# Order of the feed-forward units, layout of the attention values and place of the RWKV solve in a two-layer hybrid trunk

## The chip, the cores and the metric

The kernel runs on one core of a Trainium2 chip. The metric is the device time of one execution in microseconds (us). Three executions of the kernel before took 2157.81, 2156.45 and 2154.91 us; their median, 2156.45 us, is the time before.

The engines are named as in the profile: PE is TensorE (matmuls), PEld its weight loads, DVE is VectorE, ACT is ScalarE, POOL is GpSimd, SP is the engine that issues nearly all DMAs. Each engine takes its own instructions in a fixed order that is set when the program is built.

## The reference

Two layers; in each, two feed-forward half steps stand around a token mixer, and a small gated embedding closes the layer. The sequence has 512 tokens, the model width is 1024.

```python
def swiglu(x, w_in, w_out):                      # w_in 1024 x 5632, w_out 2816 x 1024
    gate, up = jnp.split(x @ w_in, 2, axis=-1)
    return (jax.nn.silu(gate) * up) @ w_out

# attention: 8 query heads, 2 key/value heads of 64, a window of 128 tokens, one sink logit per head
probs = jax.nn.softmax(jnp.concatenate([scores, sink], axis=-1), axis=-1)[..., :-1]
out = jnp.einsum('bnhgqk,bnkhd->bnqhgd', probs.astype(v.dtype), vb)

# RWKV-7, per token and head: S_t = S_{t-1} diag(w_t) + (S_{t-1} a_t) b_t^T + v_t k_t^T, y_t = S_t r_t

for l in range(DEPTH):
    x = x + 0.5 * rms_norm(swiglu(rms_norm(x, ln_ffn1_pre[l]), ...), ln_ffn1_post[l])
    mix = token_mixing(...)          # concat(attention, mLSTM, RWKV-7) @ w_out
    x = x + rms_norm(mix, ln_mix_post[l])
    x = x + 0.5 * rms_norm(swiglu(rms_norm(x, ln_ffn2_pre[l]), ...), ln_ffn2_post[l])
    gate = jax.nn.sigmoid(rms_norm(x, ln_ple_pre[l]) @ w_ple_gate[l])
    x = x + rms_norm(gate * (p[l] @ w_ple_proj[l]), ln_ple_post[l])
```

## The kernel before

**Precision.** A large product is three matmuls (`mm3`, L167 to L171): both factors are split into a high part (a rounding copy on ACT, L141) and the rest (a subtraction on DVE, L142), and high by high, high by low and low by high are added up. Every weight block that arrives from HBM therefore costs an ACT and a DVE pass before PE can use it.

**Feed-forward.** `ffn` (L334) computes gate and up for 22 units of 128 columns with a seven-product scheme (Strassen-Winograd over two halves of the model width and of the tokens): a unit needs sums of its weights (L386, L388, L389 on DVE), their splits (w75, w63 and w4, L390 to L392), the products 6, 7, 5, 3 and 4 on PE (L396 to L408, twelve matmuls of 128x256 each) and sums of the results on DVE (L397 to L413). The products 1 and 2, of the gate alone, are done for the first eight units (m below G = 8) ahead of all units, in `one` and `two`; for the fourteen others they stand in `gate` (L379), 24 matmuls and one more split (w12) per unit. The eight are called early units here, the fourteen late units. The loop L424 takes the units in order of their number. The result of four units fills one buffer `hs`, which `ffn_out` reads.

**Token mixing.** `weave` (L686) steps four generators in the order of the string PLAN: A attention, R the RWKV scan with its triangular solve, M the mLSTM, P the projection of its output gate. In A, `softmax` (L1360) leaves exponentials, divides them by their sum (L1387 on DVE for two heads, L1389 on POOL for the two others), and `values` (L1391) turns each block of 128 keys with four PE transposes (L1399), copies it to SBUF and multiplies: the 64 value columns are the stationary operand, the four heads' 512 columns move (L1405). The output is channel-major and is split into the high and low part for the out projection (L716 to L719). In R, `rwkv_solve` (L887) begins with `invert_merge` (L1037); its first products carry the name pt0 (L1056).

**Order.** The program is built under a scheduler that places every instruction by a simulated timeline, so neighbours in an engine's queue come from different units or generators; waits are semaphores.

## Time and profile before

| | us |
|---|---|
| median of three runs | 2156.45 |
| the profiled execution, its own time | 2158.23 |
| its span, first to last instruction | 2156.5 |
| PE busy | 2103.3 |
| PE weight loads busy | 1953.4 |
| DVE busy | 1697.9 |

The stages of the first layer in the span: feed-forward 1 to about 370 us, projections of the mixer to 500, the weave to 627, the out projection to 669, feed-forward 2 to about 1010, the gated embedding to 1080. The second layer has the same order and ends at 2156.5. The busy time of PE is a union of overlapping matmuls, so the pace of PE is read from the number of matmuls in a stretch, and its pauses from the difference between a stretch and its busy time.

### The profile page before, as it was taken

The numbers are of one execution on the slowest core, as the hardware profiler recorded it, in microseconds if no ns is written. First come the engines' busy times: TensorE is split into PE (matmuls) and PEld (weight loads), VectorE is DVE, ScalarE is ACT, GpSimd is POOL, SyncE is SP. The second block draws the span as 40 slices with busy tenths as digits, with TensorE's granted clock in tenths as the row PEclk, the third lists the DMA queues.
The fourth block names the chain that finished last, engine by engine and source line by source line (L and its number), as shares of the span: only waits on it lengthen the run. The fifth ranks groups of instructions, "written<-read, shape, count | busy, mean of one in ns | idle before, by whom it ended". The sixth has DMA issues, their size and how long they took to land.

```text
span 2156.5 us, 39845 instructions
## 1 busy us (share of the span) xinstructions
PE 2103.3 (98%) x16256; PEld 1953.4 (91%) x16256; DVE 1697.9 (79%) x2909; ACT 1015.6 (47%) x1685; POOL 219.9 (10%) x369
## 2 busy tenths in 40 slices
PE   7999999999999999999999999999999999999998
PEld 7999999898778999999889999998887789999996
DVE  8999977655767999977699999765557589999774
ACT  6444434446545444434564444345464464444343
POOL 1000011031211000011100000111412110000121
PEclk9999999999999999999999999999999999999999
DMA  5332124321042323225233222242220423222241
GB/s 215 120 116 99 70 87 153 116 65 55 21 155 71 137 99 118 69 79 182 92 108 125 111 79 93 86 169 94 61 64 2 157 88 138 100 97 79 82 147 66
DMA packets 72679, 219.10 MB, mean 102 GB/s; under 512 B 16304, under 2 KB 17328, under 8 KB 72496
## 3 DMA queue, kind: packets, MB, share of 16 engines
q1 hardware_dynamic: 72208, 216.03, 28.5%
q8 instruction: 128, 2.10, 0.4%
q10 hardware_dynamic: 288, 0.52, 0.1%
q14 instruction: 55, 0.45, 0.1%
HBM read 209.71 MB, written 6.82 MB: 100 GB/s over the span
## 4 chain that ended last, share of the span: by engine, by line
PE 84%; DVE 7%; ACT 4%; DMA 2%; issue 2%; POOL 1%; SPq 0%; DVEq 0%; POOLq 0%; ACTq 0%
PE y L496 21%; PE p L169 12%; PE p L171 12%; PE p L170 12%; PE pkrv L169 1%; PE pkrv L171 1%; PE pkrv L170 1%; DVE w L142 1%; PE y L171 1%; PE y L169 1%; PE y L170 1%; PE pgt L169 1%; PE pgt L171 1%; PE pgt L170 1%; PE po L1405 1%
## 5 line engine op out<-in xcount | busy, mean ns | idle before, releaser
L169 PE MATMUL p<-xh,w 128*128 128x256 f32 x1408 | 400.2, 286 | 14.1 <-DVE gates L397 5.8
L171 PE MATMUL p<-xh,w 128*128 128x256 f32 x1408 | 397.0, 284 | 3.7 <-DVE w L142 3.6
L170 PE MATMUL p<-xl,w 128*128 128x256 f32 x1408 | 398.7, 284 | 0.3 <-DVE xl L142 0.2
L169 PE MATMUL p<-tx,w 128*128 128x256 f32 x1056 | 294.2, 282 | 5.6 <-DVE ws L386 4.1
L170 PE MATMUL p<-tx,w 128*128 128x256 f32 x1056 | 292.1, 280 | 0.0
L171 PE MATMUL p<-tx,w 128*128 128x256 f32 x1056 | 289.8, 280 | 0.5 <-DVE w L142 0.5
L169 PEld LDWEIGHTS p<-xh,w 128*128 128x128 f32 x1408 | 268.8, 192 | 19.0 <-DVE gates L397 6.6
L171 PEld LDWEIGHTS p<-xh,w 128*128 128x128 f32 x1408 | 268.5, 192 | 5.1 <-DVE w L142 5.1
L170 PEld LDWEIGHTS p<-xl,w 128*128 128x128 f32 x1408 | 269.7, 192 | 1.0 <-DVE xl L142 0.9
L141 ACT ACTIVATE w<-ws 128x1024 fp32r<-128x1024 f32 x176 | 185.5, 1056 | 128.7 <-PE p L171 98.7
L142 DVE TENSOR_TENSOR w<-ws,w 128x1024 fp32r<-128x1024 f32 x176 | 214.0, 1217 | 19.4 <-ACT w L141 19.0
L169 PEld LDWEIGHTS p<-tx,w 128*128 128x128 f32 x1056 | 199.4, 189 | 8.1 <-ACT w L141 6.7
L170 PEld LDWEIGHTS p<-tx,w 128*128 128x128 f32 x1056 | 199.2, 189 | 0.0
L171 PEld LDWEIGHTS p<-tx,w 128*128 128x128 f32 x1056 | 196.3, 188 | 0.9 <-DVE w L142 0.7
L496 PE MATMUL y<-wo,hq 128*128 128x256 f32 x1536 | 193.3, 283 | 0.0
L496 PEld LDWEIGHTS y<-wo,hq 128*128 128x128 f32 x1536 | 186.4, 190 | 0.8
L141 ACT ACTIVATE w<-wr 128x512 fp32r<-128x512 f32 (+1 forms) x156 | 126.9, 816 | 108.8 <-PE p L171 61.5
L496 PE MATMUL y<-ws_r,h 128*128 128x256 f32 x672 | 158.3, 379 | 0.0
L142 DVE TENSOR_TENSOR w<-wr,w 128x512 fp32r<-128x512 f32 (+1 forms) x156 | 141.9, 915 | 9.9 <-ACT w L141 8.9
L532 POOL TENSOR_TENSOR tb<-tb,ln_ffn_post 128x512 f32<-128x512 f32 x16 | 24.4, 1558 | 1143.2 <-ACT junk L198 1143.2
L496 PEld LDWEIGHTS y<-ws_r,h 128*128 128x128 f32 x672 | 121.4, 189 | 13.8
L386 DVE TENSOR_TENSOR ws<-wr 128x1024 f32<-128x1024 f32 x88 | 107.0, 1216 | 0.1
(432 smaller groups left out, 4612.3 us busy)
## 6 DMA issues: line engine op xcount, KB each, us to landing
wr<-in_w_ffn_in SPq DMA_DIRECT2D x176, 512.0 KB, 4.1
ws_r<-in_w_ffn_out SPq DMA_DIRECT2D x56, 512.0 KB, 3.3
wo_r<-in_w_ffn_out SPq DMA_DIRECT2D x32, 512.0 KB, 3.3
w_r<-in_w_ffn_in SPq DMA_DIRECT2D x20, 512.0 KB, 3.8
pkrv_r<-in_w_rw SPq DMA_DIRECT2D x16, 512.0 KB, 3.5
wpg_r<-in_w_ple_gate SPq DMA_DIRECT2D x16, 512.0 KB, 4.0
xd<-x SPq DMA_DIRECT2D x8, 512.0 KB, 2.7
x<-xd SPq DMA_DIRECT2D x8, 512.0 KB, 3.5
```

The lines of the kernel that those rows point to most:

```text
L141: self.nc.scalar.activation(hi, src, AF.Copy)
L142: (eng or self.nc.vector).tensor_tensor(lo, src, hi.bitcast(F32), ALU.subtract)
L169: mm(out, a[0], b[0], start=first, stop=False, skip_group_check=shared)
L170: mm(out, a[0], b[1], start=False, stop=False, skip_group_check=shared)
L171: mm(out, a[1], b[0], start=False, stop=last, skip_group_check=shared)
L386: v_.tensor_tensor(sx.rearrange("p (i c) -> p i c", i=2), r[:, :, lo], r[:, 1].rearrange("p (i c) -> p i c", i=2), ALU.add)
L496: nc.tensor.matmul(banks[n][:, u], x, y, start=n not in seen, stop=last and i == len(todo) - 1, skip_group_check=True)
L532: (g_ if not h or QL[0] == "1" else v_).tensor_tensor(tb, tb, gain[:, h * 512:h * 512 + 512], ALU.mult)
L1405: mm(po[0][hr[g]], kv[:, t - (t + b) % 2, 2 + g], sb, start=b == 0, stop=b == nb - 1)
```

## The change

Three things change. In `ffn`, the units run in the order UNITS, which mixes early and late ones, and inside a unit the products 7 and 5 come first; the split w75 follows its sum directly. In attention, the exponentials are no longer divided: the probabilities are now the stationary operand and the 64 value columns move, one matmul per head and key block, the output is token-major, DVE multiplies it by the reciprocal sums while it leaves PSUM, and PE turns each token tile back before the split. In the RWKV solve, the first products of the first half (pt0) are issued only after the last matmul of the first tile of the mLSTM values, gates and forget gates (`pvif`).

```diff
+UNITS = (0, 1, 2, 8, 9, 3, 10, 4, 11, 12, 5, 13, 6, 14, 15, 7, 16, 17, 18, 19, 20, 21)
...
-        mm(out, a[1], b[0], start=False, stop=last, skip_group_check=shared)
+        return mm(out, a[1], b[0], start=False, stop=last, skip_group_check=shared)
...
+            w75 = self.wsplit(sx, "w75")
             v_.tensor_tensor(sy[:, lo], sx[:, hi], r[:, 0, lo], ALU.add)
             v_.tensor_tensor(sy[:, hi], sy[:, lo], r[:, 0, hi], ALU.add)
-            sx, sy = self.wsplit(sx, "w75"), self.wsplit(sy, "w63")
+            w63 = self.wsplit(sy, "w63")
...
-            product(6, self.cut(sy, lo), pc[:, L])
+            product(7, self.cut(w75, lo), pb[:, P])
+            product(5, self.cut(w75, hi), pb[:, Q])
+            product(6, self.cut(w63, lo), pc[:, L])
             v_.tensor_tensor(a[:, Q], pc[:, L], a[:, Q if m < G else P], ALU.add)
-            product(7, self.cut(sx, lo), pb[:, P])
-            product(5, self.cut(sx, hi), pb[:, Q])
...
-        for m in range(NM):
+        for m in UNITS:
...
+            if name == "pvif" and t == 0:
+                self.held = end.ins
...
-                    self.split(self.yh[:, 0:4, ts], self.yl[:, 0:4, ts], y.rearrange("p (a i) -> p a i", a=4),
-                               self.pl_(1))
+                    self.main, self.aux, self.chain = cycles["A"]
+                    pt = self.aux_tile("pat").rearrange("p (a i) -> p a i", a=4)
+                    for j in range(4):
+                        self.nc.tensor.transpose(pt[:, j], y[:, j * 128:(j + 1) * 128], self.ident)
+                    self.split(self.yh[:, 0:4, ts], self.yl[:, 0:4, ts], pt)
...
+        def first(zq):
+            if q:
+                return prod(zq, None, "pt0")
+
+            with self.tc.issue_after(self.held):
+                return prod(zq, None, "pt0")
...
-            nc.scalar.activation(t0, prod(zq, None, "pt0"), AF.Copy)
+            nc.scalar.activation(t0, first(zq), AF.Copy)
...
-            n = 4 - int(PL[4])
-            for i in range(n):
-                v_.tensor_scalar_mul(pr[:, i, :nk], pr[:, i, :nk], sm[:, i:i + 1])
-            if n < 4:
-                g_.tensor_tensor(pr[:, n:, :nk], pr[:, n:, :nk], sm[:, n:, None].to_broadcast([128, 4 - n, nk]), ALU.mult)
+            rc[g] = sm
...
-                mm(po[0][hr[g]], kv[:, t - (t + b) % 2, 2 + g], sb, start=b == 0, stop=b == nb - 1)
-            if g:
-                y = self.ytile()
-                a_.activation(y, po[0], AF.Copy)
-                ys.append(y)
+            for i in range(4):
+                for b in range(nb):
+                    mm(po[0][:, i, g], sbs[:, b, i * 128:(i + 1) * 128], kv[:, t - (t + b) % 2, 2 + g],
+                       start=b == 0, stop=b == nb - 1)
+
+            v_.tensor_tensor(ys[t].rearrange("p (a g d) -> p a g d", a=4, g=2)[:, :, g], po[0][:, :, g],
+                             rc[g][:, :, None].to_broadcast([128, 4, 64]), ALU.mult)
```

**DVE in the first feed-forward stage.** The queue of DVE from the split w75 of unit 2 on, before. The names carry buffer numbers: w75, w63, w4 and w12 are splits of weights, ws the sums of weights, wr the weights as they arrive, and gates, up and h the results of a unit.

```order
L142 TENSOR_TENSOR w75_681<-ws_676,w75_681 128x1024
L405 TENSOR_TENSOR gates_259<-p63_518,up_521 128x256
L142 TENSOR_TENSOR w63_684<-ws_677,w63_684 128x1024
L386 TENSOR_TENSOR ws_765<-wr_762 128x1024
L406 TENSOR_TENSOR up_521<-p75_519,up_521 128x256
L142 TENSOR_TENSOR w4_777<-wr_762,w4_776 128x512
L405 TENSOR_TENSOR gates_259<-p63_605,up_608 128x256
L388 TENSOR_TENSOR ws_766<-ws_765,wr_762 128x512
L409 TENSOR_TENSOR up_521<-up_521,p4_520 128x256
L397 TENSOR_TENSOR gates_259<-p63_691,gates_259 128x256
L142 TENSOR_TENSOR w75_770<-ws_765,w75_770 128x1024
```

The same place now (the lines of the changed kernel are a few numbers higher; L144 is the split, L388 the first sum):

```order
L144 TENSOR_TENSOR w75_679<-ws_676,w75_679 128x1024
L403 TENSOR_TENSOR up_608<-p75_606,gates_259 128x512
L408 TENSOR_TENSOR gates_259<-p63_518,up_521 128x256
L388 TENSOR_TENSOR ws_795<-wr_762 128x1024
L144 TENSOR_TENSOR w63_684<-ws_677,w63_684 128x1024
L409 TENSOR_TENSOR up_521<-p75_519,up_521 128x256
L144 TENSOR_TENSOR w4_807<-wr_762,w4_806 128x512
L408 TENSOR_TENSOR gates_259<-p63_605,up_608 128x256
L391 TENSOR_TENSOR ws_796<-ws_795,wr_762 128x512
L144 TENSOR_TENSOR w12_767<-wr_762,w12_767 128x1024
L412 TENSOR_TENSOR up_521<-up_521,p4_520 128x256
```

After unit 2 the weights that arrive in wr_762 were those of unit 3, an early one; now they are those of unit 8, whose split w12 for the gate's own products stands in the queue.

**PE at the first tile of pvif, first layer.** Before, the four groups of eight small transposing products pt0 stand between the first matmuls of pvif, the last of them ahead of its thirteenth (po is the attention's value product, pqt and pkt its transposes).

```order
L171 MATMUL pvif<-pvif,xl 128x264
L1050 MATMUL pt_6041<-ident,arena 64x64 x4
L1348 MATMUL pqt<-ident,arena 128x128 x4
L1050 MATMUL pt_6051<-ident,arena 64x64 x3
L169 MATMUL pvif<-pvif,xh 128x264
L1050 MATMUL pt_6051<-ident,arena 64x64 x4
L1405 MATMUL po<-arena 64x512
L1356 MATMUL pkt<-ident,arena 128x128 x2
L1050 MATMUL pt_6051<-ident,arena 64x64
L170 MATMUL pvif<-pvif,xh 128x264
```

At the same place now, none of them is left:

```order
L173 MATMUL pvif<-pvif,xl 128x264
L1363 MATMUL pqt<-ident,arena 128x128 x4
L171 MATMUL pvif<-pvif,xh 128x264
L1418 MATMUL po<-arena 128x64 x4
L1371 MATMUL pkt<-ident,arena 128x128 x2
L172 MATMUL pvif<-pvif,xh 128x264
```

The first eight stand behind the twenty-fourth matmul of pvif now, in one piece:

```order
L172 MATMUL pvif<-pvif,xh 128x264
L173 MATMUL pvif<-pvif,xl 128x264
L1058 MATMUL pt_6083<-ident,arena 64x64 x8
L171 MATMUL pvif<-pvif,xh 128x264
L172 MATMUL pvif<-pvif,xh 128x264
```

What moved is the start of the solve: past the first tile of pvif with its first eight products, and past all four tiles with the next eight, which stand behind the last matmul of pvif.

**PE at the end of the solve's first half, first layer.** Before (pz, pwt and pzq belong to the solve, pss to the mLSTM, pT and pS to attention):

```order
L1050 MATMUL pz<-arena 64x64 x16
L902 MATMUL pwt<-arena,at 64x64 x8
L1405 MATMUL po<-arena 64x512 x2
L1348 MATMUL pqt<-ident,arena 128x128 x4
L902 MATMUL pwt<-arena,at 64x64 x8
L910 MATMUL pzq<-x,arena 64x64 x16
L1196 MATMUL pss<-arena 128x128 x2
```

And now:

```order
L1058 MATMUL pz<-arena 64x64 x16
L1418 MATMUL po<-arena 128x64 x8
L1363 MATMUL pqt<-ident,arena 128x128 x4
L910 MATMUL pwt<-arena,at 64x64 x16
L918 MATMUL pzq<-x,arena 64x64 x15
L1211 MATMUL pss<-arena 128x128 x2
```

Two value matmuls of 512 columns became eight of 64, and the solve's last product pzq stands between the same neighbours as before.

## Rows read from the trace of the kernel before

**Rows 1.** The page's first and fourth part: busy time, share of the span and instructions of each engine, and the chain that ended last by engine.

```profile
PE 2103.3 (98%) x16256; PEld 1953.4 (91%) x16256; DVE 1697.9 (79%) x2909; ACT 1015.6 (47%) x1685; POOL 219.9 (10%) x369
...
PE 84%; DVE 7%; ACT 4%; DMA 2%; issue 2%; POOL 1%; SPq 0%; DVEq 0%; POOLq 0%; ACTq 0%
```

**Rows 2.** Busy time by stretch: the early units of the four feed-forward stages, then a stretch of late units. Columns: stretch, its length, then each engine's busy us and instructions, the granted clock of PE, the DMA share and GB/s.

```profile
60.00:125.00 65.00, 60.88 (x507) 60.00 (x506) 63.69 (x99) 28.54 (x36) 0.00 (x0) 1.00 0.31 115
700.00:760.00 60.00, 57.36 (x474) 56.26 (x473) 57.90 (x89) 27.45 (x33) 0.00 (x0) 1.00 0.35 126
1100.00:1190.00 90.00, 84.89 (x688) 83.62 (x689) 85.69 (x126) 42.84 (x58) 0.00 (x0) 0.98 0.34 124
1766.00:1835.00 69.00, 67.11 (x557) 66.09 (x556) 67.38 (x101) 32.29 (x40) 0.00 (x0) 1.00 0.38 138
162.00:216.00 54.00, 54.00 (x457) 54.00 (x456) 50.34 (x76) 24.62 (x33) 0.00 (x0) 1.00 0.27 99
```

**Rows 3.** Who PE waited for in the stretch 60 to 125 us: us in total, times, longest.

```profile
PE p L169 <- DVE ws L386: 1.9, 1, 1.9
PE p L169 <- DVE gates L397: 1.4, 1, 1.4
PE p L171 <- DVE w L142: 0.8, 1, 0.8
```

**Rows 4.** Busy time by stretch: the weave of the first and of the second layer; columns as in rows 2.

```profile
500.00:626.90 126.90, 120.69 (x1234) 95.62 (x1232) 84.10 (x270) 67.26 (x176) 24.51 (x28) 0.99 0.11 35
1568.20:1691.30 123.10, 121.02 (x1225) 94.42 (x1224) 82.55 (x264) 66.37 (x175) 22.75 (x27) 0.99 0.11 32
```

**Rows 5.** Who PE waited for in the weave of the first layer.

```profile
PE pwt L1182 <- DVE arena L1224: 1.2, 1, 1.2
PE pst L954 <- POOL arena L948: 1.0, 1, 1.0
...
PE py L962 <- DVE x L911: 0.6, 1, 0.6
PE pT L1399 <- DVE arena L1387: 0.6, 1, 0.6
```

**Rows 6.** The timeline of DVE in the stretch 60 to 125 us: start, duration, line and operation.

```profile
82.14 0.68 DVE L389 TENSOR_TENSOR ws<-ws,wr 128x512 f32<-128x512 f32 x1
82.74 1.22 DVE L386 TENSOR_TENSOR ws<-wr 128x1024 f32<-128x1024 f32 x1
83.87 0.41 DVE L397 TENSOR_TENSOR gates<-p,gates 128x256 f32<-128x256 f32 x1
84.21 0.41 DVE L409 TENSOR_TENSOR up<-up,p 128x256 f32<-128x256 f32 x1
```

**Rows 7.** Groups of DVE splits: count, then busy us and mean ns of one, then the idle time of DVE just before them and what ended it.

```profile
L142 DVE TENSOR_TENSOR w<-ws,w 128x1024 fp32r<-128x1024 f32 x176 | 214.0, 1217 | 19.4 <-ACT w L141 19.0
L142 DVE TENSOR_TENSOR w<-wr,w 128x512 fp32r<-128x512 f32 (+1 forms) x156 | 141.9, 915 | 9.9 <-ACT w L141 8.9
```

**Rows 8.** Busy time by stretch around a pause of PE in the second layer, then the same pause in the first layer; columns as in rows 2.

```profile
1148.00:1151.00 3.00, 1.10 (x9) 0.90 (x8) 3.00 (x6) 1.38 (x2) 0.00 (x0) 1.00 0.11 26
1151.00:1154.40 3.40, 3.40 (x18) 3.40 (x18) 3.38 (x6) 0.00 (x0) 0.00 (x0) 0.51 0.72 286
82.00:85.40 3.40, 1.50 (x13) 1.44 (x13) 3.40 (x6) 1.06 (x1) 0.00 (x0) 1.00 0.41 149
```

**Rows 9.** The timeline of PE at one pair of value products: start, duration, line, operation and shape.

```profile
547.15 1.93 PE L1405 MATMUL po<-arena 128*64 128x512 f32 x4
549.01 0.33 PE L1348 MATMUL pqt<-ident,arena 128*128 128x128 f32 x1
```

**Rows 10.** Groups of the attention's instructions that go, and the nearest one to what comes on DVE; columns as in rows 7.

```profile
L1405 PE MATMUL po<-arena 128*64 128x512 f32 x56 | 27.5, 605 | 0.0
L1387 DVE TENSOR_SCALAR arena<-arena,sm 128x256 f32<-128x256 f32 (+1 forms) x32 | 17.8, 598 | 0.3
L1389 POOL TENSOR_TENSOR arena<-arena,sm 128x512 f32<-128x512 f32 (+1 forms) x16 | 15.7, 980 | 111.6 <-DVE sm L1384 74.6 <-DVE vg L1118 35.5 <-ACT ysq L989 1.5
L405 DVE TENSOR_TENSOR gate<-p,up 128x256 f32<-128x256 f32 x56 | 23.4, 417 | 7.5 <-PE p L171 7.4
```

**Rows 11.** The timeline of PE's weight loads at a matmul of 16 columns (pgm) and at the projection after it.

```profile
532.24 0.30 PEld L1132 LDWEIGHTS pgm<-vg,arena 128*128 128x128 f32 x2
532.46 0.19 PEld L170 LDWEIGHTS pog<-pog,xh 128*128 128x128 f32 x1
532.57 0.19 PEld L171 LDWEIGHTS pog<-pog,xl 128*128 128x128 f32 x1
```

**Rows 12.** The chain of waits in the weave of the first layer: one group of four transposes there.

```profile
544.38 0.59 PE pT L1399 x4
```

**Rows 13.** The timeline of DVE just ahead of the first wait of rows 5; columns as in rows 6.

```profile
559.10 1.40 DVE L1387 TENSOR_SCALAR arena<-arena,sm 128x256 f32<-128x256 f32 x2
560.42 0.48 DVE L1224 COPY arena<-pnum 128x130 f32<-128x130 f32 x2
```

**Rows 14.** The timeline of PE at the solve's start in the first layer, pt0 and the products after it; columns as in rows 9.

```profile
502.15 0.45 PE L1050 MATMUL pt<-ident,arena 64*64 64x64 f32 x8
...
509.58 0.44 PE L1050 MATMUL pgi<-arena,x 64*64 64x64 f32 x6
520.48 1.02 PE L1050 MATMUL pgi<-arena,x 64*64 64x64 f32 x26
```

More of the change, by code (lines that the diff above doesn't have):

```diff
@@ L345, in ffn @@
         right = {1: plain(k1, L), 2: plain(k2, L), 3: plain(k2, H), 4: tx[2], 5: plain(k1, H), 6: tx[0], 7: tx[1]}
-        hs = []
+        hs = {}
         lo, hi = slice(0, 512), slice(512, 1024)
@@ L403, in unit @@
                 v_.tensor_tensor(a[:, P], pa[:, H], a[:, P], ALU.add)
-            product(3, self.cut(sy, hi), pc[:, H])
+            product(3, self.cut(w63, hi), pc[:, H])
             v_.tensor_tensor(a[:, Q], pc[:, H], b[:, Q], ALU.add)
@@ L409, in unit @@
             v_.tensor_tensor(b[:, P], b[:, P], pd[:, L], ALU.subtract)
-            if m % 4 == 0:
-                hs.append(self.slot("h", [8, 256], "h"))
+            if m // 4 not in hs:
+                hs[m // 4] = self.slot("h", [8, 256], "h")
             v_.scalar_tensor_tensor(hs[m // 4][:, m % 4 * 2:m % 4 * 2 + 2], b.rearrange("p (i t) -> p i t", i=2), -1.0,
@@ L608, in tm_proj @@
                 for i in range(w[0].shape[1] // cols):
-                    self.mm3(ps[:, t % two], [q[:, k, t * 128:(t + 1) * 128] for q in (self.xh, self.xl)],
+                    end = self.mm3(ps[:, t % two], [q[:, k, t * 128:(t + 1) * 128] for q in (self.xh, self.xl)],
                              [q[:, i * cols:(i + 1) * cols] for q in w], k == 0, k == 7)
                     k += 1
+            if name == "pvif" and t == 0:
+                self.held = end.ins
             if t % two == two - 1:
@@ L1394, in values @@
             if g == 0:
-                po[0] = self.mm_tile("po")
+                po[0] = self.mm_tile("po").rearrange("p (a g d) -> p a g d", a=4, g=2)
+                ys.append(self.ytile())
             for b in range(nb):
@@ L1399, in values @@
                     tr(pT[:, i], pr[:, i, b * 128:(b + 1) * 128], self.ident)
-                sb = sbs[:, b]
                 if b:
-                    v_.tensor_copy(sb, pT.rearrange("p a i -> p (a i)"))
+                    v_.tensor_copy(sbs[:, b], pT.rearrange("p a i -> p (a i)"))
                 else:
-                    a_.activation(sb, pT.rearrange("p a i -> p (a i)"), AF.Copy)
-                mm(po[0][hr[g]], kv[:, t - (t + b) % 2, 2 + g], sb, start=b == 0, stop=b == nb - 1)
-            if g:
-                y = self.ytile()
-                a_.activation(y, po[0], AF.Copy)
-                ys.append(y)
+                    a_.activation(sbs[:, b], pT.rearrange("p a i -> p (a i)"), AF.Copy)
+            for i in range(4):
[4 more added lines that the diff above has]
+                             rc[g][:, :, None].to_broadcast([128, 4, 64]), ALU.mult)
         po = [None]
+        rc = {}
         self.ys = ys = []
```

## The prediction

> **What bounds the kernel now.** I read the page first: PE is busy for 2103.3 of 2156.5 us, and the chain that ended last is PE for 84% [rows 1]. So only two things can move the time: the 53 us in which PE is idle, and the work that PE is given. Next the busy time by stretch, to see where the idle time lies. In late units PE makes 457 matmuls in 54.0 us without a gap, 0.118 us each, with DVE busy for 50.3; in the stretches of the early units PE is idle for 4.1, 2.6, 5.1 and 1.9 us while DVE is busy for 93 to 98% [rows 2]. The list of waits names DVE, and each wait is one that stands behind other DVE work: the sums and splits of the next weights, or L397, which reads a result before PE may go on in that bank [rows 3]. In the two weaves PE is idle for 6.2 and 2.1 us [rows 4], behind DVE and once POOL [rows 5].
>
> **The units.** One DVE instruction starts 0.60 us (512 columns), 1.13 us (1024) or 0.34 us (256) after the one before it [rows 6]. An early unit has three of 1024 (L386 and two splits), five of 512 (L388, L389, the split w4, L400, L413) and four of 256 (L397, L405, L406, L409): 3.39 + 3.00 + 1.36 = 7.75 us, against 60 matmuls x 0.118 = 7.08 us on PE. A late unit adds the split w12 and L403 on DVE, 9.22 us, and 24 matmuls on PE, 9.91 us. An early unit puts DVE 0.67 us behind, a late one 0.69 us ahead.
> Eight early units in a row put DVE 8 x 0.67 = 5.4 us behind. The four stretches lost 4.12 + 2.64 + 5.11 + 1.89 = 13.8 us, 3.4 a stage [rows 2], so DVE came in with a lead of 2.0 us. In the new order the debt is 2.0 after units 0, 1, 2, falls to 0.6 after 8 and 9, and never passes 2.0 again (1.3 after unit 3 and so on): with the same lead nothing is left to wait for. DVE also idles for ACT's half of a split, 29.3 us over 88 units, 0.33 each [rows 7]. Harmless where PE binds, it counts where DVE does; then an early unit costs 1.00, a late one returns 0.36, the debt before was 8.0, the lead 4.6, and the new debt is largest at unit 7, with eight early and eight late units done: 8.0 - 2.9 = 5.1, so that 0.5 a stage stays. I take 0.7 a stage, a little above both, since both engines now run at the limit for sixteen units: 13.8 - 2.8 = 11.0 us gained.
> The new order of products helps the same way: product 7 needs only the first sum and its split, where product 6 waited for three sums. I price it at nothing beyond this.
> One of the pauses is followed by a half clock: after 1.9 us without matmuls PE is granted 0.51 for 3.4 us, the lower of its two levels (1.2 of 2.4 GHz), while the same pause in the first layer leaves the clock at 1.00 [rows 8]. If the pause goes, half of 3.4 goes, 1.7 us. Together 12.7. Bounds: 0, if the waits only move, and 13.8 + 1.7 = 15.5.
> DMAs: the same 512 KB blocks in another order through the same three slots; the DMA share is 0.27 to 0.38 [rows 2], so I add nothing.
>
> **The values.** Before, one pair of key blocks holds PE from 547.15 to 549.01, 1.86 us for four passes (each f32 matmul is two); half of it for the first tile. Per layer 6 x 1.86 + 2 x 0.93 = 13.0 us, 26.0 in both, near the 27.5 of the group [rows 9, 10]. Now there are 56 matmuls a layer, 112 passes, each with a weight load of 128 columns. Two such loads with only 16 columns to multiply start 0.11 us apart, as do the loads after them [rows 11]. So 112 x 0.11 = 12.3 us, less by 0.7. The sixteen transposes of the output are new, 16 x 0.11 = 1.8. Net +1.1 a layer, +2.2.
> Bounds: the old product moves 512 columns per pass in 1.86 / 4 = 0.465 us, so 64 columns alone would take 0.058; 112 x 0.058 = 6.5 and the net is -4.7 a layer, -9.4. Upwards, four transposes span 0.59 us with their start [rows 12], 0.148 each; 128 x 0.148 = 18.9, +5.9 a layer, +11.8. I take the pitch of the loads, measured on the very shape.
> The page "TensorE: Matmul & The Clock Gate" of the Trainium skill, section "Back-to-back issue gap", gives about 60 cycles for an isolated matmul of up to 64 columns, which would be 25 ns a pass, 2.8 us a layer, and would make the sum lower by another 19 us. The same section says that loads and matmuls together set the spacing; the 0.11 of the trace agrees with that and not with the table, so the table stays a rival.
> DVE loses 32 L1387 (17.8 us) and gains 16 products from PSUM like L405 (0.42 us, 6.7); POOL loses 15.7 us [rows 10]. ACT loses eight copies and the splits stay. None of these engines binds: DVE has 84.1 of 126.9 us in the weave [rows 4]. What counts are waits: two L1387, 1.40 us, stand straight ahead of the copy L1224 that PE waited 1.2 for [rows 5, 13]; PE waited 0.6 for L1387 itself and 0.6 for L911. These 2.4 us go, in the first layer; the 1.0 for POOL's copy L948, which follows L911, stays in both. Bounds: 0 and 6.2, all that PE idles there. What is late next is the scan's own chain.
>
> **The solve.** pt0 goes behind the first tile of pvif. Instead of standing in pieces between matmuls it now stands in one. The products pgi that need it ran at 509.58 and 520.48 [rows 14]; the later ones are not moved, and by the order the solve's last product keeps its neighbours. Cover: the gate projection, which PE does between. I take 0; bounds -1 (fewer switches) and +21.8 (below).
>
> **The sum.** 2158.2 (the profiled execution's own time) - 12.7 + 2.2 - 2.4 = 2145.3 us. That execution stands 1.8 above the median, so 2143.5, rounded to **2143 us**.
>
> **The rivals.**
> Moved stalls. Sixteen units now ask DVE for 8 x 7.75 + 8 x 9.22 = 135.8 us and PE for 135.9, so every hiccup of one is a wait of the other, where before late units let DVE catch up. For it: DVE at 98% already in the first stretch [rows 2]. Against it: the largest debt falls from 5.4 to 2.0, or from 8.0 to 5.1. If it keeps half of the stalls and the half clock, 6.9 - 2.2 + 2.4 = 7.1 is gained: 2149.
> Columns set the pace. If a pass of 64 columns takes 0.058 us, as the old product's columns do, the values give 9.4 in place of costing 2.2: 2132. For it: a pass of 64 columns has an eighth of the columns that the old one had. The table of the Trainium skill points the same way, further down. Against it: the loads 0.11 apart [rows 11].
> Slower: the solve's delay. The earliest pgi goes from 509.58 to where the later ones stood, 520.48 [rows 14]: 10.9 us. If the serial chain solve, scan, last block of the out projection sets the end of the weave, each layer ends 10.9 us later: +21.8 - 12.9 = +8.9, 2165. It decides once the solve's last product starts over 6.5 us later than before in both layers, where the gain of 12.9 is gone. For it: the scan is serial and the out projection needs its last output. Against it: most of pgi stood at 520.48 before, too.
> No gain: the waits of the units move wholly, and the attention's 2.2 and 2.4 cancel: 2156.
>
> **How the numbers follow.** Forecast 0.58 (its own range 2137 to 2149), columns 0.08, moved stalls 0.16, no gain 0.09, slower 0.09. A measurement of this kernel can tell about 0.2%, 4.3 us, from no change. Faster by more: 0.58 + 0.08 + 0.15 = 0.81; within 0.2%: 0.09 + 0.01 = 0.10; slower 0.09. The range from 2131 to 2156 leaves out the slower case, half of no gain and the far end of columns.
>
> **What would show it.** In the changed kernel's stretches of the first sixteen units PE should idle for about 1 us a stage, with DVE near 98% throughout, and no half clock near 1151 us less the shift. The loads of the value products should start 0.11 us apart, and sixteen transposes a layer take 1.8 us. No wait for L1387 or L1224 should be left in the weave. The stretch from the first pvif matmul to the end of the weave should be no longer than before by more than 1 us. I am wrong if PE idles for over 2 us a stage, if the loads come closer than 0.07, or if the solve's last product starts more than 6.5 us later.

## The result and the profile after

The changed kernel takes 2143.0 us (median of six executions, 2138.5 to 2144.5), the kernel before 2156.9 beside it (six, 2152.4 to 2158.4). The ratio is 0.9937, 95% interval 0.9925 to 0.9948: 13.9 us less. The forecast was 2143.

The page of the changed kernel, its first line and its first and fourth part, answers to [rows 1].

```profile
span 2142.5 us, 40293 instructions
PE 2097.8 (98%) x16456; PEld 1969.6 (92%) x16456; DVE 1683.6 (79%) x2893; ACT 1013.0 (47%) x1681; POOL 204.3 (10%) x353
PE 85%; ACT 5%; DVE 5%; DMA 3%; issue 2%; POOL 1%; SPq 0%; DVEq 0%; POOLq 0%; ACTq 0%
```

The span is 14.0 us shorter and PE is idle for 44.7 us where it was idle for 53. Busy time by stretch of the changed kernel, in the first sixteen units of each stage (as in [rows 2]) and in the two weaves ([rows 4]); columns: stretch, length, each engine's busy us and instructions, granted clock, DMA share, GB/s.

```profile
60.00:120.00 60.00, 59.58 (x499) 59.17 (x498) 57.55 (x88) 28.55 (x38) 0.00 (x0) 1.00 0.29 107
700.00:762.00 62.00, 62.00 (x524) 62.00 (x523) 59.89 (x91) 28.79 (x37) 0.00 (x0) 1.00 0.31 111
1100.00:1184.00 84.00, 83.69 (x700) 83.14 (x699) 80.35 (x118) 38.93 (x52) 0.00 (x0) 1.00 0.32 116
1760.00:1835.00 75.00, 75.00 (x632) 75.00 (x631) 72.52 (x109) 34.09 (x43) 0.00 (x0) 1.00 0.35 125
...
497.30:627.00 129.70, 126.44 (x1372) 110.17 (x1370) 79.75 (x264) 68.37 (x176) 16.23 (x21) 1.00 0.14 42
1557.90:1689.20 131.30, 128.07 (x1372) 111.63 (x1370) 79.94 (x264) 68.60 (x176) 16.20 (x21) 0.99 0.14 42
```

Where 13.8 us were idle in the units, 0.7 are left, and the half clock near 1151 is gone. The weaves still have 3.3 and 3.2 us (before 6.2 and 2.1), but none of the waits of [rows 5] is among them:

```profile
PE pS L1385 <- ACT ng L1171: 0.9, 1, 0.9
PE pvif L171 <- ACT pvif L143: 0.7, 1, 0.7
PE pS L1385 <- DVE parts L1366: 0.4, 1, 0.4
...
```

The value products and the new transposes on PE's timeline: eight passes fill the 0.94 us from 502.62 to the next instruction, 0.117 each with the first; over a layer 112 passes take 12.6 us, 0.1125 each, and the sixteen transposes 1.9.

```profile
502.62 1.10 PE L1418 MATMUL po<-arena 128*128 128x64 f32 x8
503.56 0.39 PE L1371 MATMUL pkt<-ident,arena 128*128 128x128 f32 x2
...
596.60 1.05 PE L726 MATMUL pat<-ident,yt 128*128 128x128 f32 x8
597.48 0.61 PE L1243 MATMUL pc<-vg,mg 128*128 128x130 f32 x4
```

So most marks that the prediction had set are met: the pauses of the units, the half clock, the distance of the passes, the waits. DVE stands at 96 to 97% in the first sixteen units, where 98 was said. One mark is missed: from the first pvif matmul to the end of the weave the first layer takes 127.7 us where it took 124.3 (the second 129.2 and 130.5). And cut into stages by the starts of PE's matmuls, the 14.0 us are made up otherwise than the sum of the prediction: the first sixteen units give 14.2 (567.1 to 552.9 over the four stages), the mixers 7.3, and 7 to 8 are lost again: 2.9 at the starts of the stages (products 1 and 2 of units 0 to 7), 1.8 in the last six units, 2.0 in the down projections, the rest in smaller pieces. A stretch of half clock less stands in each of the 14.2 and the 7.3, by an estimate 1.7 us each (half of 3.4). The experiments ask which part does what.

### The profile page after: what moved, and what is told of

Read it like the earlier page. It is cut to its first block, busy times and chain, and to the rows that moved or that the text cites. A ratio compares the mean times of both kernels' runs of the same rounds, so it can differ in the third digit from the quotient of the medians.

```text
span 2142.5 us, 40293 instructions
## 1 busy us (share of the span) xinstructions
PE 2097.8 (98%) x16456; PEld 1969.6 (92%) x16456; DVE 1683.6 (79%) x2893; ACT 1013.0 (47%) x1681; POOL 204.3 (10%) x353
## 3 DMA queue, kind: packets, MB, share of 16 engines
q1 hardware_dynamic: 72208, 216.03, 29.4%
## 4 chain that ended last, share of the span: by engine, by line
PE 85%; ACT 5%; DVE 5%; DMA 3%; issue 2%; POOL 1%; SPq 0%; DVEq 0%; POOLq 0%; ACTq 0%
PE y L499 20%; PE p L171 13%; PE p L173 13%; PE p L172 13%; PE pkrv L173 1%; PE pkrv L172 1%; PE pkrv L171 1%; PE y L171 1%; PE y L172 1%; PE y L173 1%; PE po L1418 1%; PE pgt L172 1%; PE pgt L173 1%; PE pgt L171 1%; DMA w_r<-in_w_ffn_in 1%
## 5 line engine op out<-in xcount | busy, mean ns | idle before, releaser
L144 DVE TENSOR_TENSOR w<-ws,w 128x1024 fp32r<-128x1024 f32 x176 | 214.8, 1222 | 10.5 <-ACT w L143 10.1
L143 ACT ACTIVATE w<-wr 128x1024 fp32r<-128x1024 f32 (+1 forms) x156 | 127.1, 816 | 134.5 <-PE p L173 79.2
L144 DVE TENSOR_TENSOR w<-wr,w 128x1024 fp32r<-128x1024 f32 (+1 forms) x156 | 142.7, 920 | 12.6 <-ACT w L143 12.0
L499 PEld LDWEIGHTS y<-ws_r,h 128*128 128x128 f32 x672 | 121.0, 189 | 15.2 <-DMA ws_r<-in_w_ffn_out 1.3
L388 DVE TENSOR_TENSOR ws<-wr 128x1024 f32<-128x1024 f32 x88 | 107.4, 1221 | 0.0
```

What stands on the lines that cost most here:

```text
L143: self.nc.scalar.activation(hi, src, AF.Copy)
L144: (eng or self.nc.vector).tensor_tensor(lo, src, hi.bitcast(F32), ALU.subtract)
L388: v_.tensor_tensor(sx.rearrange("p (i c) -> p i c", i=2), r[:, :, lo], r[:, 1].rearrange("p (i c) -> p i c", i=2), ALU.add)
L499: nc.tensor.matmul(banks[n][:, u], x, y, start=n not in seen, stop=last and i == len(todo) - 1, skip_group_check=True)
```

## The experiments

Each version was timed against the kernel before on its own chip; the difference is of medians, the interval is that of the ratio. "Start" is the time of the 192 matmuls at the start of the second feed-forward half step, in layers 1 and 2; "mixer" the time from the last projection matmul (pqk) to the last of the out projection; an asterisk marks a stretch with 3.4 us of half clock in it (by an estimate 1.7 us lost). Start, mixer and pauses are those of the one profiled execution of a version. "Pauses" are the distances between successive starts of matmuls above the median of their form, from 0.15 us up, in the first sixteen units of all four stages. All three are worked out from PE's timeline. The first row is the kernel before.

| version | median, us | less than before | 95% of ratio | start | mixer | pauses |
|---|---|---|---|---|---|---|
| before | 2156.9 | | | 27.6, 32.0* | 166.0*, 164.0* | 15.3 |
| order UNITS alone | 2149.7 | 5.2 | 0.9963 to 0.9984 | 27.5, 27.6 | 163.7, 165.3* | 11.6 |
| product order alone | 2149.3 | 5.7 | 0.9961 to 0.9983 | 27.5, 27.5 | 163.7, 165.3* | 8.9 |
| both (feed-forward part) | 2144.9 | 11.4 | 0.9931 to 0.9956 | 27.5, 27.5 | 163.7, 163.7 | 5.8 |
| values alone | 2150.4 | 5.9 | 0.9958 to 0.9983 | 30.1, 29.9 | 159.6, 163.2* | 13.6 |
| held solve alone | 2151.4 | 4.9 | 0.9968 to 0.9988 | 27.4, 27.8 | 161.4, 161.4 | 15.2 |
| values and held | 2149.9 | 6.5 | 0.9956 to 0.9977 | 30.1, 30.1 | 160.6, 160.6 | 13.6 |
| feed-forward and held | 2137.8 | 17.1 | 0.9907 to 0.9932 | 27.5, 27.5 | 162.3*, 161.4 | 5.8 |
| feed-forward and values | 2140.2 | 14.7 | 0.9919 to 0.9944 | 32.2*, 29.6 | 159.5, 159.5 | 3.4 |
| whole change | 2143.0 | 13.9 | 0.9925 to 0.9948 | 31.7*, 30.6 | 160.6, 162.1* | 3.4 |
| whole, rows in order | 2139.5 | 17.2 | 0.9910 to 0.9937 | 27.4, 29.0 | 160.8, 160.9 | 5.8 |
| feed-forward, values, rows | 2136.1 | 20.5 | 0.9892 to 0.9919 | 27.4, 29.3 | 159.9, 160.4 | 5.8 |
| the same, units spread | 2137.9 | 18.8 | 0.9903 to 0.9933 | 27.4, 29.4 | 160.0, 159.7 | 3.5 |

**The feed-forward part, and its halves.**

```diff
+UNITS = (0, 1, 2, 8, 9, 3, 10, 4, 11, 12, 5, 13, 6, 14, 15, 7, 16, 17, 18, 19, 20, 21)
-        for m in range(NM):
+        for m in UNITS:
```

> The kernel before with the order UNITS alone; inside a unit the products stay 6, 7, 5 and both splits stay behind the third sum. Prediction's theory (debt of DVE in early units, product order worth nothing): the same as the whole feed-forward part, which measured 11.4 us less: 2145. Rival: product 6 first still waits for three sums and for L397 behind it, and the product order carries part of the gain: 3 to 6 us slower than the whole feed-forward part, 2148 to 2151.

```diff
+            w75 = self.wsplit(sx, "w75")
...
-            product(6, self.cut(sy, lo), pc[:, L])
+            product(7, self.cut(w75, lo), pb[:, P])
+            product(5, self.cut(w75, hi), pb[:, Q])
+            product(6, self.cut(w63, lo), pc[:, L])
```

> The kernel before with products 7 and 5 first and the early split of w75, units still 0 to 21 in order. Prediction's theory: DVE's debt of eight early units in a row is as before, so 0, 2156. Rival: the stalls of the early units go with the product order (product 7 needs one sum and one split only), 4 to 8 us less, 2148 to 2152.

Both edits together:

> The kernel before with the feed-forward part of the change alone: the order UNITS, products 7 and 5 first, w75 split directly after its sum. Prediction's theory (the units term is what made the time): 12.7 us less than before, 2144, and the mixer's weave as long as before. Rival, from the trace of the changed kernel by stretches: the stretches of the first sixteen units give 14.2 us, but 6.5 come back at the starts of the stages (the first two products of units 0 to 7: 122.2 against 119.3 us over four stages) and behind the sixteenth unit, so 7 to 8 us less, 2149. A second rival, that the waits only move: 0.

The whole part gives what the units term said (11.4 of 12.7), but not by its reason. Of the 15.3 us of pauses in the kernel before the order of units alone removes 3.7, the product order alone 6.4, both 9.5; in time the two halves are equal within the noise (5.2 and 5.7). In length the first sixteen units of the version with the order of units alone take 567.6 us, no less than before (two stretches of half clock in place of one make 1.7 of that by estimate), and its last six 3.2 more; its profiled execution took 2155.2 us, and the 5.2 of the median is not traced to a stage. With the units alone the longest pause of [rows 3], about 2 us, does not go: it moves from 81.8 to 104.75 us, in front of unit 4, where the debt, four early and three late units, is 0.6 or 2.9 by the two counts of the prediction, below its leads of 2.0 and 4.6. That version's answer to who PE waited for there, then DVE's timeline and ACT's, with the idle time ahead in brackets:

```profile
PE p L171 <- DVE ws L388: 1.9, 1, 1.9
```

```profile
99.30 1.23 DVE L144 TENSOR_TENSOR w<-ws,w 128x1024 fp32r<-128x1024 f32 x1
101.94 1.23 DVE L144 TENSOR_TENSOR w<-ws,w 128x1024 fp32r<-128x1024 f32 x1 [1.41 <-ACT w L143]
```

```profile
100.85 1.06 ACT L143 ACTIVATE w<-ws 128x1024 fp32r<-128x1024 f32 x1 [1.58 <-issue]
105.82 1.06 ACT L143 ACTIVATE w<-ws 128x1024 fp32r<-128x1024 f32 x1 [0.84 <-DVE ws L391]
```

Three to five us before PE stops, DVE idles for 1.41 us and ACT for 1.58: neither is out of throughput there. PE starts at 106.92, when ACT has finished the split that product 6 needs first (105.82 + 1.06 = 106.88); that split stood behind three sums. The releaser that is named, L388, happens to end at the same moment. It is a chain of split, sums and ACT's half of the next split that is late. It begins at PE: no view names what ACT's 1.58 us wait for, but in the trace ACT stands at semaphores of DVE and PE until 100.80, and at 100.76 PE ends a product that reads a split. A wait for one of the three buffers of the splits (NW) fits that; no run changed their number. Product 7 has a shorter chain, since it needs one sum and one split, and that is what the product order should buy.

The longest pause of the kernel before looks otherwise: ahead of it DVE works without a gap from 58.9 to 84.6 us (its last rows are [rows 6]). There the debt of the prediction is not refuted.

With the product order alone part of the gain goes into the next stage: its pauses in the down projections rise from 14.2 to 21.3 us, and the waits named there are for DMA. Who PE waited for in its first down projection:

```profile
PE y L497 <- DMA ws_r<-in_w_ffn_out: 1.4, 1, 1.4
```

**The values and the solve.** The first edit, the last lines of the diff of the change without the solve:

```diff
-                mm(po[0][hr[g]], kv[:, t - (t + b) % 2, 2 + g], sb, start=b == 0, stop=b == nb - 1)
...
+                    mm(po[0][:, i, g], sbs[:, b, i * 128:(i + 1) * 128], kv[:, t - (t + b) % 2, 2 + g],
+                       start=b == 0, stop=b == nb - 1)
```

> The kernel before with token-major attention values alone. Prediction's theory: +2.2 us for the passes, -2.4 for the waits that go in the first weave, together -0.2, so 2156 to 2157, no change that can be measured. Rival: the relief of DVE and POOL is worth more than two waits, and what the weaves lost in the changed kernel (5.4 and 1.9 us) comes from here: 5 to 7 us less. The value passes should start 0.112 us apart in either case (12.6 us a layer) and the sixteen transposes take 1.9 us a layer.

```diff
+            with self.tc.issue_after(self.held):
+                return prod(zq, None, "pt0")
```

> The kernel before with the solve's first products queued behind the first tile of pvif, nothing else. Prediction's theory: 0 (bounds -1 and +21.8). Rival that the changed kernel's trace suggests: the solve's small products (pt, pgi, pz, pzq) took 2.3 and 1.7 us less time on PE once they stand together, so 4 us less; if the delay of the solve costs, more than before.

Both:

> The kernel before with the values and the held solve, and the old feed-forward. By stretches of the changed kernel's trace: the two mixers were 7.3 us shorter, so 7 us less than before, 2150; by the prediction: 0 to 0.2 less, 2156.5. If the parts add up, this and the feed-forward part together make the 13.8 us of the whole change, and the single parts of the mixer make this one.

The prediction's sum fell in both. Values: po takes 12.6 to 12.7 us as before and the transposes 1.9, so +1.9 a layer, near the +1.1 of the prediction; but the mixer gets 4.2 shorter, in both layers (163.7 to 159.5 with the new feed-forward), so some 6 come from elsewhere. PE's idle time gives 3.4 of them: 5.0 us with the new feed-forward and the old values, 1.5 with the new ones (columns as above, the first layer of each). Another 1.5 lie in pgi and pt, small products of the solve that start closer together; the rest is in pieces.

```profile
498.20:627.00 128.80, 123.84 (x1252) 97.51 (x1251) 84.95 (x272) 68.07 (x179) 24.50 (x28) 1.00 0.15 44
499.10:625.00 125.90, 124.38 (x1356) 108.46 (x1355) 77.40 (x260) 66.55 (x175) 16.22 (x21) 1.00 0.14 43
```

Who PE waited for in the first weave of these two, in the same order:

```profile
PE pst L957 <- POOL arena L951: 1.0, 1, 1.0
PE y L171 <- ACT xh L143: 0.9, 1, 0.9
PE pnum L1212 <- POOL rs L181: 0.7, 1, 0.7
PE pT L1402 <- DVE arena L1390: 0.6, 1, 0.6
PE py L965 <- DVE x L914: 0.6, 1, 0.6
...
```

```profile
PE pmb L1152 <- ACT vg L1151: 0.4, 1, 0.4
PE pS L1376 <- DVE parts L1357: 0.4, 1, 0.4
...
```

The 1.0 for POOL that the prediction kept, the wait of the out projection for a split and that for POOL's rs are gone too. That they went because DVE and POOL have less to do is not shown: in the second layer of the kernel before, with the old attention, PE idles for 2.1 us only [rows 4], and of the five waits of the first list only the 1.0 for POOL is there. Which waits stand in a weave also hangs on how the scheduler placed it, and no run holds that fixed.

The held solve alone is worth 2.3 us a layer in the mixer (161.4 against 163.7). Its products pt take 4.5 us in 7 unbroken pieces in place of 5.7 in 12, and with the values 4.8 in 9 and 5.1 in 10: 0.24 us for each piece. All its small products together (pt, pgi, pz, pwt, pzq) take 21.2 us a layer in place of 23.4, about what the mixer gains; but they lie in 45 pieces either way, so the price of a piece holds for pt alone. The first 32 matmuls of pt on PE's timeline, in the feed-forward version without the held solve and with it (there the first piece lies in a stretch of half clock, 503.9 to 507.3 us):

```profile
498.98 0.45 PE L1053 MATMUL pt<-ident,arena 64*64 64x64 f32 x8
501.03 0.45 PE L1053 MATMUL pt<-ident,arena 64*64 64x64 f32 x8
501.99 0.44 PE L1053 MATMUL pt<-ident,arena 64*64 64x64 f32 x6
502.87 0.45 PE L1053 MATMUL pt<-ident,arena 64*64 64x64 f32 x8
504.62 0.32 PE L1053 MATMUL pt<-ident,arena 64*64 64x64 f32 x2
```

```profile
506.34 1.12 PE L1055 MATMUL pt<-ident,arena 64*64 64x64 f32 x16
517.23 0.68 PE L1055 MATMUL pt<-ident,arena 64*64 64x64 f32 x16
```

Beside the values the mixer is 1.0 us a layer longer with it, 160.6 against 159.6: PE idles for 3.3 us there again in place of 1.5. In time the loss shows with the rows in order (17.2 less than before against 20.5), hardly in the whole change (13.9 against 14.7), and not without the new feed-forward (6.5 against 5.9).

**With the feed-forward part.** The held solve, then the values, are put on it by the edits above.

> The feed-forward part and the held solve, without the token-major values. If parts add: 11.4 + 4.9 = 16.3 us less than before, 2140, and so below the whole change (2143). The two small products of units 0 to 7 at the start of the second feed-forward half step should take 27.5 us in each layer, as without the values. Prediction's theory (the values cost 2.2 and give back 2.4, the held solve is 0): 2144 to 2145.

> The feed-forward part and the token-major values, without the held solve. If parts add: 11.4 + 5.9 = 17.3 us less, 2139. Rival: the values end the rows of the out projection bunched together, so that the start of the second feed-forward half step takes 30 to 31 us in place of 27.5 in each layer, which the old unit order half absorbed and the new one doesn't; then 8.2 us gained in the weaves less 6 at these starts, 2142 to 2144, about the whole change. Prediction's theory: 2145.

Without the values the parts add (17.1 against 16.3), and this version is 3.2 us faster than the whole change (17.1 against 13.9 below the kernel before). With them 2.6 of 17.3 are lost. The column "start" shows where: 27.4 to 27.8 us in every changed version without the values, 29.6 to 32.2 in every one of the table with them and the rows as they come. The kernel before has both: 27.6 in its first layer, 32.0 in its second.

**The rows of the out projection.** In the second half of the out projection four tiles of 128 tokens get 24 matmuls each. In every changed version without the values the tiles end one after the other, 5.5 us apart. With them the matmuls of three tiles alternate; they do so in the second layer of the kernel before, too, but in its first layer not. In the whole change these tiles end at 646.2, 648.7 and 652.6 us, while the stage behind begins at 661.0. The edit queues each tile behind the one before, and the first two then end at 641.9 and 647.4:

```diff
+                with self.tc.issue_after(end) if h and t else nullcontext():
-                for i, w, a in rest:
-                    one(i, w, a, t)
+                    for i, w, a in rest:
+                        end = one(i, w, a, t)
```

> The changed kernel with the second half of the out projection kept in the order of its rows: the products of one tile of 128 tokens are queued behind those of the tile before (in the changed kernel those of three tiles alternate). Theory: the alternation is what makes the start of the second feed-forward half step slow, since the rows come to the norm bunched; in order, the first two products of units 0 to 7 take 27.5 us in place of 31.7 and 30.6, so 5 to 7 us less than the changed kernel, 2136 to 2138. Rival: the tiles alternate because the blocks of the out projection's weights come late, so PE now waits for them and nothing is gained: 2142 to 2145. Rival: the slow start comes from the changed attention itself (its splits on ACT and DVE at the end of the weave), so the start stays at 30 us or more: 2142 to 2144.

> Feed-forward part, token-major values and the out projection in the order of its rows, without the held solve. By the runs so far the held solve adds 1.0 us a layer to the weave beside the values, so 1 to 2 us below the run with it, 2134 to 2137, and below the version without the values (2138). If the held solve is worth what it is worth alone (4.9 us), slower than the run with it by that.

The whole change gains 3.3 us by it (17.2 against 13.9) where 5 to 7 were forecast. The starts fall from 31.7 and 30.6 to 27.4 and 29.0, 5.9 us of which an estimated 1.7 are clock, and nothing is lost in the mixer; but the first sixteen units take 2.7 more, since pauses return there (3.4 to 5.8, see below). So the alternation is what makes the start slow, in the first layer wholly and in the second in part; the rival of late weights fell. In the whole change the third group of transposes of the next stage comes at 665.81 and 666.73, 5 us after the stage's first product at 661.03, in two pieces, and ACT later stands for a weight block (PE's and ACT's timeline):

```profile
665.81 0.60 PE L222 MATMUL xtp<-ident,xn 128*128 128x128 f32 x4
666.73 0.60 PE L222 MATMUL xtp<-ident,xn 128*128 128x128 f32 x4
```

```profile
678.28 1.06 ACT L143 ACTIVATE w<-w_r 128x1024 fp32r<-128x1024 f32 x1 [3.06 <-DMA w_r<-in_w_ffn_in]
```

The second layer of the kernel before, whose rows alternate without the values, shows the same two marks behind its first product at 1735.19:

```profile
1739.96 0.60 PE L220 MATMUL xtp<-ident,xn 128*128 128x128 f32 x4
1740.88 0.60 PE L220 MATMUL xtp<-ident,xn 128*128 128x128 f32 x4
...
1752.72 1.06 ACT L141 ACTIVATE w<-w_r 128x1024 fp32r<-128x1024 f32 x1 [3.37 <-DMA w_r<-in_w_ffn_in]
```

So the single versions without the values gain some 2.5 us on the kernel before at this start, beside what their own part does: its 32.0 are 30.3 without the clock, theirs 27.5 to 27.8.

Who PE waited for in that start, in the whole change and with the rows in order, and the timeline of the latter, whose stage begins at 661.0 too:

```profile
PE p L171 <- ACT gates L367: 1.3, 3, 0.6
PE p L171 <- ACT w L143: 1.2, 1, 1.2
PE p L173 <- DVE w L144: 0.8, 1, 0.8
...
```

```profile
PE p L171 <- ACT xh L143: 0.5, 1, 0.5
PE p L173 <- DVE w L144: 0.3, 1, 0.3
...
```

```profile
661.91 1.32 PE L222 MATMUL xtp<-ident,xn 128*128 128x128 f32 x8 [0.28 <-DVE xn L211]
```

With the values and the rows and no held solve the kernel takes 2136.1 us, the lowest median: 20.5 less than before. Its interval overlaps that of the feed-forward part and the held solve (17.1 less).

**The price of a value pass.**

```diff
+                for c in range(0, 64, 32):
...
+                        mm(po[0][:, i, g, c:c + 32], sbs[:, b, i * 128:(i + 1) * 128],
+                           kv[:, t - (t + b) % 2, 2 + g, c:c + 32], start=b == 0, stop=b == nb - 1)
```

> The changed kernel with each value product cut into two of 32 columns with the same stationary probabilities: twice the passes and twice the weight loads, the same number of columns in all. If the load of 128 columns sets the pace (prediction's theory, 0.11 us a pass), 112 more passes a layer cost 12.6 us, 25.2 in both: 2168. If the columns set it (the rival of the prediction), nothing is added: 2143. If it is the table's fixed 25 ns for a pass of up to 64 columns: 224 x 0.025 = 5.6 us more, 2149.

```profile
503.01 1.97 PE L1419 MATMUL po<-arena 128*128 128x32 f32 x16
504.81 0.41 PE L1371 MATMUL pkt<-ident,arena 128*128 128x128 f32 x2
```

Sixteen passes of 32 columns fill 1.80 us, 0.1125 each: half the columns, the same distance. So at 32 and 64 moving columns a pass with its load has the same price, and both the columns and the table fall. That the load sets it, and not another fixed price of a pass, fits but is not shown: no run changed the columns of the load. The Trainium skill, "TensorE: Matmul & The Clock Gate", section "LDWEIGHTS (loading the stationary operand)", gives the columns of the load over 1.2 in ns, by which 128 would take an estimated 107. The trace's 112.5 stands 5% above that. The time was no test: 2224.6 us, ratio 1.0302 to 1.0344, some 82 above the change and not 25. By estimate the passes are 25.2 of it and granted half clocks 37.5 (81.9 us at half speed against 6.8, half of each lost); the other 19 are waits that were not followed up.

**Where the early units stand.** On the fastest version:

```diff
-UNITS = (0, 1, 2, 8, 9, 3, 10, 4, 11, 12, 5, 13, 6, 14, 15, 7, 16, 17, 18, 19, 20, 21)
+UNITS = (0, 1, 2, 8, 9, 10, 3, 11, 12, 4, 13, 14, 5, 15, 16, 6, 17, 18, 7, 19, 20, 21)
```

> The fastest version so far (feed-forward part, token-major values, out projection in the order of its rows, no held solve: 2136.1) with the early units spread over all 22 units instead of the first sixteen: after 0, 1, 2 each early unit has two or three late ones before it. Prediction's theory (the debt of DVE, 0.67 or 1.00 an early unit, less 0.69 or 0.36 a late one, makes the pauses): the debt falls after every group, and of the 5.8 us of pauses in the units of the four stages, of which 1.2 in each of two stages stand at unit 2 or 3, at least 2 more go: 2134. Rival, from the traces: a pause is the chain sum, ACT's half of a split, DVE's half, PE of one unit, in which DVE itself idles, and the debt is not what counts: the pauses stay at 5 to 6 us and the time at 2135 to 2138. Third: early units late in the stage disturb the down projection behind them: over 2139.

2137.9, no better. Over all 22 units the pauses are 6.7 us against 6.5: those of the first sixteen fall from 5.8 to 3.5 and those of the last six rise by as much. So the forecast of the debt, 2 us less, fell. The pause of 1.18 us at 14 us into the units of the second half steps stays where it is, in both layers. It is no test of the debt, since both orders are the same up to there, and it has a cause of its own: ahead of its Silu (L412) ACT loads a table, 1.28 us, and this load stands between two splits. In the fastest version PE starts again at 703.61, when the second of them is done by 0.05 us; the whole change has the same load behind its splits, at 15.0 us into the units in place of 12.7, and no pause. ACT's timeline in the first and in the second of these:

```profile
699.61 1.06 ACT L143 ACTIVATE w<-ws 128x1024 fp32r<-128x1024 f32 x1 [3.78 <-PE p L173]
700.69 1.28 ACT L412 ACT_TABLE_LOAD   x1
...
702.52 1.04 ACT L143 ACTIVATE w<-ws 128x1024 fp32r<-128x1024 f32 x1
```

```profile
705.99 1.06 ACT L143 ACTIVATE w<-ws 128x1024 fp32r<-128x1024 f32 x1 [1.75 <-PE p L173]
...
707.75 1.28 ACT L410 ACT_TABLE_LOAD   x1
```

All six versions with products 7 and 5 first whose rows come in order have this pause, and the three whose rows alternate do not. Twice 1.18 is the 2.4 between 5.8 and 3.4 in the column of pauses. No run moved the load by itself.

## Why the prediction was right, and where it was not

The time was right, 2143.0, and in part by luck, since errors of the sum cancelled. In the trace of the whole change the units' stretches give 14.2 and the rest of these stages takes 3.8 back, where 12.7 was forecast; the mixers give 7.3 where values and solve were to give 0.2; the starts, which the sum did not have, cost 2.9.

- **The units, 12.7.** Alone the part measures 11.4, and the whole change has 0.7 us idle in these stretches against the 2.8 that I left. What failed is part of the working: "I price it at nothing beyond this" for the product order, which by itself removes more of the pauses (6.4) than the order of units (3.7). The debt balances busy times. That fits the longest pause of the kernel before, ahead of which DVE has no gap, but not the one that the order of units leaves, with DVE and ACT idle ahead of it, nor the two of 1.18 us behind a table load. (The DVE shares of the early stretches in [rows 2] are 95 to 98%; the 93 is that of the late one. Nothing hangs on it.) What the prediction did not ask is what becomes of the time: the down projections and the last units took back 3.8 in the whole change.
- **The passes, +2.2.** Right in mechanism and nearly in size: 0.1125 us a pass against 0.11, transposes 0.119 each; +3.7 in place of +2.2, about half of the difference since po had cost 12.65 us a layer and not 13.0. Columns as the pace are refuted.
- **The waits of the weave, −2.4.** Mis-sized. The old list of PE's waits was read as a fixed set from which two lines go. In fact the values alone shorten each mixer by 4.2 us net of the +1.9 that they cost, about 6 a layer and 12 in both, of which PE's idle time is 3.4 a layer. Whether the relief of DVE and POOL does it or the other placing of the weave stays open, since in the second layer of the kernel before PE idles for only 2.1 us without it.
- **The solve, 0, bounds −1 and +21.8.** Alone −4.9, outside the bounds: the solve's small products take 2.2 us a layer less, which was not priced (1.2 of it in pt, which lies in 7 pieces in place of 12), and the second layer's start is 2.5 shorter. On top of the values the mixer is 1.0 a layer longer. The delay did not come: the last pzq starts at 594.0 us, before 598.1, though the projections ended only 2.7 us sooner.
- **What the sum lacked.** The start of the second feed-forward half step: 27.6 and 32.0 us in the kernel before, 31.7 and 30.6 in the whole change, 27.4 and 29.0 with the rows in order. Of the 22 us that the three parts give singly (11.4 + 5.9 + 4.9), 13.9 are left. These starts are some 6 of the 8 by estimate (with 1.7 off for a half clock: 3.5 less than before, added over the single runs, and 2.7 more in the whole change); the mixers are another 3 (in the same way 8.5 less and 5.6 less).
- **The rivals.** For the order of units alone the time is that of moved stalls (2149.7), and its longest pause moves; for the whole that rival is wrong. The solve's delay and no gain did not come. The mark "first pvif to the end of the weave" was useless: it failed in the first layer although the mixer is 5.4 us shorter (1.7 of it clock by estimate), since the out projection now begins 10 us earlier and fills PE there.

What stays open: why the rows alternate in some versions (the scheduler's timeline sets it, and the second layer of the kernel before shows that the values are not needed for it), why the second layer's start keeps 1.5 us of the loss with the rows in order, and what more buffers for the splits would do.

## What to carry to other kernels

Where PE waits for a prepared operand, count the chain to the first product (sums, splits, engines in turn) before the balance of busy times: an order of products that begins with the one that is ready first removed more of the pauses here than an order of units, though in time the two were equal. Look at what else stands in that chain: a buffer to be given back, or a table load on ACT between two splits. Judge a part of a change also by the stage behind it, since the faster part can bunch up what the next stage reads; and time the parts singly and together, since a forecast that hits can hide errors that cancel. Where a scheduler places the program, look at both layers of the kernel before: what a change seems to bring may stand there already.

## What the hardware showed unexpectedly

With passes of 32 columns PE was granted half clock for far longer than in any other run. The stretch before the longest such piece, and that piece:

```profile
1655.00:1660.20 5.20, 3.53 (x32) 2.81 (x30) 3.78 (x18) 3.08 (x11) 0.47 (x2) 1.00 0.01 3
1660.30:1691.00 30.70, 30.70 (x197) 27.24 (x196) 10.95 (x40) 6.70 (x23) 2.40 (x4) 0.50 0.00 1
```

After 5.2 us with 32 matmuls PE stays at the lower of its two levels (1.2 of 2.4 GHz) for 30.7 us, in which the profile counts it busy throughout. The Trainium skill, "TensorE: Matmul & The Clock Gate", section "What's actually happening", has activity release the throttle; this row does not show it. In the other runs a piece at half clock lasted 3.4 us, at the end of the kernel 5 to 9, and it stood at other places in each execution: 601, 1151, 1622 and 1755 us in the profiled one before, 681 and 1599 in that of the change. So by an estimate of half of each piece 3.4 of the 14.0 us between these two spans are clock.
